# A fourth raw tile beside the gates, one-hot rows for four tokens at a time, and accumulating transfers for every second unit of the selection

## The chip, the cores and the metric

One core of one Trainium2 chip runs the whole program. The metric is the device time of one execution in microseconds, the median of the runs. The engines are named as in the profile: PE (TensorE, its matrix multiplications; PEld its weight loads), DVE (VectorE), ACT (ScalarE), POOL (GpSimd) and SP (SyncE, which issues most transfers). A transfer runs on the DMA engines; it is issued by a queue of SP or POOL.

## The reference

Two network blocks run over 256 tokens of width 1024 in fp32. The part that the change touches is the PEER layer, which occurs twice ("peer0", "peer1"):

```python
q = (xt @ w_q).reshape(T, 8, 2, 128)
s = jnp.einsum('thcd,hcnd->thcn', q, sub_keys)            # scores against 128 keys, two halves
s1, i1 = lax.top_k(s[:, :, 0], 16)
s2, i2 = lax.top_k(s[:, :, 1], 16)
cand_s = (s1[..., :, None] + s2[..., None, :]).reshape(T, 8, 256)
top_s, top_pos = lax.top_k(cand_s, 16)                    # 16 of 16384 experts per head and token
gates = jax.nn.softmax(top_s, axis=-1)
act = gelu(einsum('thkd,td->thk', u[expert_idx], xb))
out = einsum('thk,thkd->td', gates * act, v[expert_idx])
```

The other stages (an mLSTM mixer, latent attention, two feed-forward layers, a mixing layer of retention and neighbourhood attention) compute in fp32 as well.

## The kernel before

**Dense experts.** The kernel does not gather experts. For each of the 128 blocks of 128 experts it multiplies all 256 tokens with the block's u (`block(b)`, L499), applies gelu and stores the result in "big" (128 experts by 128 blocks by 256 tokens). A matrix of gates, zero where an expert is not chosen, is multiplied into "big", and the product with all of v (L556) is the output.

**Three passes.** Each fp32 product is made of three matmuls of fp32r parts: a number is split into a high part ("hi", a cast on ACT, L449) and the rest ("lo", a subtraction, L450). In a u-block, 16 matmuls read the high part of the weights and then 8 read the low part, so hi is needed about 1.9 us before lo.

**The stream of weights.** `Stream` carries all weights through the program in units of 128x1024 numbers (512 KB). `load` (L268) issues the transfer of a unit into a raw tile ("wraw", three of them) on SP's queue. `prep` makes hi and lo of it, two blocks ahead of use, in three pairs of tiles. The subtraction runs on DVE, or on POOL for units in `on_pool`. For a unit in `on_dma` there is no subtraction: `begin` (L300) lets ACT write the negated raw unit into one of two spare tiles (L306, tile "x1" or a name beginning with x), and POOL issues an accumulating transfer (L307) that adds the same unit from memory, in pieces: the copy is rounded to fp32r, so what is left in the tile is lo; the cast to hi follows in `prep` (L295). `fill` decides how far ahead that is begun, and `load_ahead` how far ahead is loaded:

```python
for i in range(self.done, self.done + (3 if self.done + 2 in self.borrow else 1)):
    if i in self.on_dma and i not in self.begun:
        self.begin(i)
...
while self.loaded < min(self.n, self.done + self.raw + (len(self.lent_raws) if self.loaded in self.borrow else 0)):
    self.load(self.loaded)
```

`lend` gives the stream more raw tiles for a range of units (`borrow`): in the selection, four pieces of "big" not yet written, for 44 units.

**One PEER layer.** First come 16 query units (`s_query`, `s_score`; in peer0 13 of them have their subtraction on POOL). Then 128 u-blocks run on PE, and beside them, on DVE, first the selection of the experts: `select` is a generator that yields the cost of each piece, and `spend(steps, 1.6)` lets each block take pieces up to that budget. When it is through, `Gates` starts in the same block (L943 to L949): `Gates.upto` calls `Gates.step` 67 times, spread evenly over the blocks that are left. A step joins the gates of four tokens to the finished blocks on DVE (L1688), makes one-hot rows in f16 on DVE (`make`, L1665 to L1668, four operations of 128x1024 for eight tokens, every second step, in one of two "hot" tiles), multiplies them on PE (`product`, L1678, eight matmuls for four tokens; two products after each other, every second step), and writes the gates of the blocks still to come on ACT (L1692). For the tokens whose gates are already in "big", gelu of a new block goes to a tile of its own, "gl" and a quarter of "x0" in turn (L1053), and DVE multiplies it in (`joins`, L1061); the other tokens go straight into "big" (L1056).

**Order.** DVE's instructions run in the order in which the code writes them. On PE, ACT, POOL and SP a planner with its own costs sets the order ahead of time, by due times and by what it thinks is ready; it is not the order of the code. `keep_in_program_order` ties an instruction behind the one before it in the code on the same engine.

Of the kernel before, what the change touches and what calls it, by code (L numbers as in the profile page):

```python
# [19 lines left out]
P = 128  # L20
# [18 lines left out]
FF_TAIL = 6  # L39
PACE = 4  # L40

SELECT, LENT = 44, 4

GATE_SCALE = 2.0 ** 15

# [183 lines left out]
class Stream:  # L229
# [38 lines left out]
    def load(self, i):  # L268
        n, w = (i - self.borrow.start) % (self.raw + len(self.lent_raws)) - self.raw, self.widths[i]
        t = self.lent_raws[n] if i in self.borrow and n >= 0 else self.tile(i, "raw", F32, self.raw)  # L270
        self.k.nc.sync.dma_start(out=t[:, :w], in_=self.src[i, :, :w])
        self.raws[i] = t

    def ring(self, i):
# [80 lines left out]
class Net:  # L355
# [292 lines left out]
    def mlstm(self, gain):  # L648
        nc, v, tc = self.nc, self.nc.vector, self.tc
        mm = nc.tensor.matmul  # L650
        with tc.tile_pool(name="ml", bufs=1) as pool, self.in_order():
# [196 lines left out]
                        (nc.gpsimd if ti else v).tensor_tensor(gog[:, ti], gog[:, ti], hng, op=ALU.mult)  # L848

            stages = [lambda h: None, s_decay, s_scores, s_turn, s_out, s_norm, s_keep]  # L850
            self.w.on_pool.update(range(self.w.i + 12, self.w.i + 40))
            for step, todo in enumerate(ML_BESIDE):
                todo = list(todo)
                if step == 2:
# [32 lines left out]
    def peer(self, layer, gain):  # L887
        nc, v, tc = self.nc, self.nc.vector, self.tc
        mm = nc.tensor.matmul
        with tc.tile_pool(name="pr", bufs=1) as pool:  # L890
# [20 lines left out]

            first = self.w.i + 16
            self.w.lend([self.room(big, n) for n in range(14, 14 + LENT)], range(first, first + SELECT))
            self.w.on_dma = set(range(self.w.i + 16 + 1, self.w.i + 16 + P - 8, 3))

            sc = self.scores_of(big)
            st = {}
# [22 lines left out]
            def block(b):  # L940
                ps = self.pp.tile([P, 512], F32, tag="acc", name=self.nm("ub"), bufs=4)
                self.cols_late(ps, self.xT, self.w.next())
                gates, start = now["gates"], now["start"]  # L943
                if start is not None:
                    gates.upto(b - 1, Gates.STEPS / (P - 2 - start))
                elif spend(steps, 1.6):
                    inner.close()
                    gates.pool = inner.enter_context(tc.tile_pool(name="gt", bufs=1))
                    now["start"] = b  # L949
                if b == P - 2:  # L950
                    gates.rest(b - 1)
                self.joins(late)
                if now["last"]:
                    self.activate(big, gates, late, *now["last"])
                now["last"] = b, ps
# [91 lines left out]
    def activate(self, big, gates, late, b, ps):  # L1047

        nc = self.nc
        t0 = gates.tokens if gates else 0  # L1050
        if t0:
            y = self.t(gates.pool, [P, S], "gl") if b % 2 else gates.room
            nc.scalar.activation(y[:, :t0], ps[:, :t0], AF.Gelu)  # L1053
            late.append((big[:, b, :t0], y[:, :t0]))
        if t0 < S:
            nc.scalar.activation(big[:, b, t0:], ps[:, t0:S], AF.Gelu)  # L1056
# [581 lines left out]
class Gates:  # L1638
# [1 line left out]

    TB = 8
    TJ = 4
    MADE = S // TB
    GROUPS = S // TJ
# [2 lines left out]
    def __init__(self, k, big, idx, g, iota):  # L1649
        self.k, self.big, self.idx, self.g = k, big, idx, g  # L1650
        x0 = k.t(k.gp, [P, 8, P, 2], "x0", F16)
        self.room = x0[:, 6:].rearrange("p a b c -> p (a b c)").bitcast(F32)
        self.iota, self.q = x0[:, self.TB // 2], x0[:, :self.TB // 2]
        k.nc.scalar.copy(self.iota, iota.unsqueeze(2).to_broadcast([P, P, 2]))
        self.pool = None
        self.tokens, self.n, self.owed = 0, 0, 0.0
        self.made, self.ps = {}, {}

    def make(self, m):
        k, tt, n = self.k, self.k.nc.vector.tensor_tensor, self.TB // 2  # L1660
        t = slice(m * self.TB, (m + 1) * self.TB)
        hot = k.t(self.pool, [P, 3, n, P, 2], "hot", F16, bufs=2)
        iota = self.iota.unsqueeze(1).to_broadcast([P, n, P, 2])
        on = lambda x: x[:, t].rearrange("p (a b) -> p a b", a=n).unsqueeze(2).to_broadcast([P, n, P, 2])
        tt(hot[:, 0], iota, on(self.idx[1]), op=ALU.is_equal)  # L1665
        tt(self.q, iota, on(self.idx[0]), op=ALU.is_equal)
        for p in range(2):
            tt(hot[:, 1 + p], self.q, on(self.g[:, p]), op=ALU.mult)  # L1668
        self.made[m] = hot
# [11 lines left out]
    def join(self, g, blocks, done):  # L1681
# [5 lines left out]
        if done and blocks:  # L1687
            nc.vector.scalar_tensor_tensor(dst, ps[:, :blocks], 1.0 / GATE_SCALE, dst, op0=ALU.mult, op1=ALU.mult)  # L1688
        if not done:
            assert self.k.w.done >= self.k.w.borrow.stop  # L1690
            if blocks < P:
                nc.scalar.mul(dst, ps[:, blocks:], 1.0 / GATE_SCALE)  # L1692
            self.tokens = (g + 1) * TJ
            self.ps.pop(g)

    def step(self, blocks):
        n = self.n
        self.n += 1
        join = 0 <= n - 3 < self.GROUPS
        if join:  # L1700
            self.join(n - 3, blocks, True)
        m, odd = divmod(n, self.TB // self.TJ)
        if m < self.MADE and not odd:
            self.make(m)
        if not odd:
            for g in (n - 2, n - 1):
                if 0 <= g < self.GROUPS:
                    self.product(g)
        if join:
            self.join(n - 3, blocks, False)  # L1710

# [11 lines left out]
def spend(steps, budget):  # L1723

    while budget > 0:
        c = next(steps, False)
        if c is False:
            return True
        if c is None:
            return False  # L1730
        budget -= c
    return False
# [59 lines left out]
```

## Time and profile before

| | |
|---|---|
| Median of 3 runs | 2618.07 us (2617.72 to 2621.56) |
| The profiled execution | 2626.37 us, span 2624.6 us |
| PE busy | 2551.2 us, 97% of the span |
| DVE busy | 1749.5 us, 67% |
| ACT busy | 1329.1 us, 51% |
| POOL busy | 259.6 us, 10% |

The profiled execution is 8.3 us longer than the median. Busy shares are an average over stages with different limits, so the stages are read one by one. For peer0 they are, in us from the start: the query stage 152.25 to 215.96; u-blocks 0 to 11, 215.96 to 251.21; blocks 12 to 35, 251.21 to 327.69; blocks 36 to 46, 327.69 to 359.97; blocks 47 to 127, in which gates are made, 359.97 to 633.15. In peer1 the query stage is 1133.12 to 1192.90 and blocks 47 to 127 are 1336.89 to 1611.59.

How to read the views: a timeline row is the start in us, the duration, engine, line and operation, out<-in with the shape, and how many consecutive ones the row joins; in brackets stands the idle time before it and what ended it. A row of the waits is the engine, tile and line that waited, for whom, the sum in us, how often, and the longest. A row of the groups has the count behind x, then busy time, mean ns of one, idle time before them and what ended it. A matmul's end is modelled, so that rows of PE overlap a little: starts are what to subtract. Some matmul records can be missing.

### The profile page before, as it was taken

The numbers are of one execution on the slowest core, as the hardware profiler recorded it, in microseconds if no ns is written. First come the engines' busy times: TensorE is split into PE (matmuls) and PEld (weight loads), VectorE is DVE, ScalarE is ACT, GpSimd is POOL, SyncE is SP. The second block draws the span as 40 slices with busy tenths as digits, with TensorE's granted clock in tenths as the row PEclk, the third lists the DMA queues.
The fourth block names the chain that finished last, engine by engine and source line by source line (L and its number), as shares of the span: only waits on it lengthen the run. The fifth ranks groups of instructions, "written<-read, shape, count | busy, mean of one in ns | idle before, by whom it ended". The sixth has DMA issues, their size and how long they took to land. (4 is left out here: it accounts for less than half of the span.)

```text
span 2624.6 us, 42853 instructions
## 1 busy us (share of the span) xinstructions
PE 2551.2 (97%) x16706; PEld 2303.7 (88%) x16706; DVE 1749.5 (67%) x3116; ACT 1329.1 (51%) x2109; POOL 259.6 (10%) x227
## 2 busy tenths in 40 slices
PE   8999999999999998999999999999999999999999
PEld 7789999999888887889999999888887998887898
DVE  6878966677555567679966677555566546666654
ACT  5445555555444445545555555444445444564543
POOL 0552000000000003010000000000011003001000
PEclk9999999999999999999999999999999999999999
DMA  7356777776555564367867776555565654554653
GB/s 246 109 194 194 217 194 209 209 203 223 201 192 193 193 207 159 118 204 206 224 186 201 206 211 224 194 193 193 193 201 192 223 162 169 180 178 153 208 194 105
DMA packets 139195, 502.42 MB, mean 191 GB/s; under 512 B 15832, under 2 KB 16088, under 8 KB 138992
## 3 DMA queue, kind: packets, MB, share of 16 engines
q1 hardware_dynamic: 122832, 443.93, 49.7%
q0 software_dynamic: 15440, 54.64, 11.1%
q8 instruction: 131, 2.15, 0.3%
q10 hardware_dynamic: 720, 1.11, 0.1%
q14 instruction: 72, 0.59, 0.1%
HBM read 494.38 MB, written 5.24 MB: 190 GB/s over the span
## 5 line engine op out<-in xcount | busy, mean ns | idle before, releaser
L450 DVE TENSOR_TENSOR wlo<-wraw,whi 128x1024 fp32r<-128x1024 f32 x446 | 547.1, 1228 | 499.2 <-ACT whi L449 498.2
L449 ACT CAST whi<-wraw 128x1024 fp32r<-128x1024 f32 x488 | 510.1, 1047 | 522.0 <-PE acc L556 319.9
L499 PE MATMUL ub<-xT,whi 128*128 128x256 f32 x4096 | 540.2, 285 | 4.6 <-ACT whi L449 4.4
L556 PE MATMUL acc<-whi,xT 128*128 128x512 f32 x1816 | 510.3, 394 | 12.3 <-ACT whi L449 7.3
L499 PEld LDWEIGHTS ub<-xT,whi 128*128 128x128 f32 x4096 | 507.9, 191 | 7.4 <-ACT whi L449 7.0
L556 PEld LDWEIGHTS acc<-whi,xT 128*128 128x128 f32 x1816 | 342.8, 190 | 85.9 <-ACT whi L449 7.3
L450 DVE TENSOR_TENSOR morelo<-wraw,morehi 128x1024 fp32r<-128x1024 f32 (+1 forms) x214 | 261.7, 1227 | 115.5 <-ACT morehi L449 115.1
L449 ACT CAST morehi<-wraw 128x1024 fp32r<-128x1024 f32 (+1 forms) x227 | 236.8, 1047 | 177.4 <-DMA wraw<-in_wst 71.6
L556 PE MATMUL acc<-wlo,xT 128*128 128x512 f32 x908 | 284.0, 393 | 0.2 <-DVE wlo L450 0.2
L556 PE MATMUL acc<-morehi,xT 128*128 128x512 f32 x808 | 234.2, 390 | 0.6 <-ACT morehi L449 0.6
L499 PE MATMUL ub<-xT,wlo 128*128 128x256 f32 x1408 | 200.2, 285 | 8.5 <-DVE wlo L450 8.0
L556 PEld LDWEIGHTS acc<-wlo,xT 128*128 128x128 f32 x908 | 172.5, 190 | 37.1 <-DVE wlo L450 0.9
L499 PEld LDWEIGHTS ub<-xT,wlo 128*128 128x128 f32 x1408 | 181.0, 191 | 13.3 <-DVE wlo L450 13.0
L556 PEld LDWEIGHTS acc<-morehi,xT 128*128 128x128 f32 x808 | 151.2, 188 | 32.3 <-ACT morehi L449 1.4
L450 POOL TENSOR_TENSOR wlo<-wraw,whi 128x1024 fp32r<-128x1024 f32 (+1 forms) x42 | 100.6, 2398 | 709.7 <-ACT whi L449 705.0
L455 PE MATMUL ps<-xT,whi 128*128 128x256 f32 (+1 forms) x552 | 160.9, 292 | 0.0
L456 PE MATMUL ps<-xT,whi 128*128 128x256 f32 (+1 forms) x552 | 159.2, 289 | 0.4 <-DVE xT L450 0.4
L457 PE MATMUL ps<-xT,wlo 128*128 128x256 f32 (+1 forms) x552 | 158.8, 288 | 0.0
L307 POOL DMA_DIRECT2D x<-in_wst x80 | 68.9, 862 | 759.2 <-ACT big L1056 228.7
L306 ACT ACTIVATE x<-wraw 128x1024 fp32r<-128x1024 f32 x64 | 67.8, 1060 | 138.7 <-DMA wraw<-in_wst 138.6
L556 PE MATMUL acc<-morelo,xT 128*128 128x512 f32 x404 | 128.4, 390 | 0.8 <-DVE morelo L450 0.8
L457 PE MATMUL ps<-xT,morelo 128*128 128x256 f32 x416 | 118.2, 284 | 2.3 <-POOL morelo L450 1.7
(498 smaller groups left out, 4213.6 us busy)
## 6 DMA issues: line engine op xcount, KB each, us to landing
wraw<-in_wst SPq DMA_DIRECT2D x768, 512.0 KB, 4.0
x<-in_wst POOLq DMA_DIRECT2D x80, 512.0 KB, 5.5
big<-in_wst SPq DMA_DIRECT2D x48, 512.0 KB, 5.3
wraw<-in_wst SPq DMA_DIRECT2D x10, 384.0 KB, 3.3
sp<-x SPq DMA_DIRECT2D x4, 512.0 KB, 3.0
big<-in_keys POOLq DMA_DIRECT2D x8, 256.0 KB, 7.5
sp<-big SPq DMA_DIRECT2D x4, 512.0 KB, 7.7
x<-sp POOLq DMA_DIRECT2D x4, 512.0 KB, 4.8
```

The costliest lines, as they stand in the source:

```text
L306: k.nc.scalar.mul(lo[:, :w], self.raws[i][:, :w], -1.0)
L307: k.nc.gpsimd.dma_start(out=lo[:, :w], in_=self.src[i, :, :w], accum_op=ALU.add)
L449: self.nc.scalar.copy(hi, src)
L450: (self.nc.gpsimd if pool else self.nc.vector).tensor_tensor(lo, src, hi.bitcast(F32), op=ALU.subtract)
L455: mm(ps, a[0], b[0], start=start, stop=False)
L456: mm(ps, a[0], b[1], start=False, stop=False)
L457: mm(ps, a[1], b[0], start=False, stop=stop)
L499: mm(ps[:, :S], w[of][:, k], xT[part][:, k], start=n == 0, stop=n == len(steps) - 1)
L556: mm(acc[ti][h], a, w[b][:, h * 512:(h + 1) * 512], start=first, stop=last)
```

## The change

In the selection, every second unit instead of every third gets its lo by an accumulating transfer (20 units of the first 40, then 27, so 47 instead of 40 per layer); the four lent tiles serve 40 units instead of 44, and a block takes pieces of the selection up to a budget of 1.75. In the gates' stretch a new tile "wraw" is lent as a fourth raw tile, for all units up to the end of u; since `fill` looks at `borrow`, accumulations may there be begun up to three units ahead. One-hot rows are made for four tokens in each step (four operations of 128x512, in one of three tiles), and one product follows each step. "gl" is replaced by a second quarter of "x0", which smaller one-hot rows leave free; the tile sizes add up to the same. All transfers of `load` are tied to program order on SP. In the query stage of peer0 the subtractions that POOL did move to DVE: the range for POOL ends with the mLSTM's own units.

```diff
-SELECT, LENT = 44, 4
+SELECT, LENT = 40, 4
...
-        self.k.nc.sync.dma_start(out=t[:, :w], in_=self.src[i, :, :w])
+        self.k.tc.keep_in_program_order(self.k.nc.sync.dma_start(out=t[:, :w], in_=self.src[i, :, :w]))
...
-            self.w.on_pool.update(range(self.w.i + 12, self.w.i + 40))
+            self.w.on_pool.update(range(self.w.i + 12, self.until))
...
-            self.w.on_dma = set(range(self.w.i + 16 + 1, self.w.i + 16 + P - 8, 3))
+            self.w.on_dma = set(range(first + 1, first + SELECT, 2)) | set(range(first + SELECT + 1, first + P - 8, 3))
...
-                elif spend(steps, 1.6):
+                elif spend(steps, 1.75):
                     inner.close()
                     gates.pool = inner.enter_context(tc.tile_pool(name="gt", bufs=1))
                     now["start"] = b
+                    gates.lent = first + SELECT
+                    raw = self.t(gates.pool, [P, UNIT], "wraw")
+                    self.w.lend([raw], range(max(self.w.loaded, first + SELECT), first + P))
...
-            y = self.t(gates.pool, [P, S], "gl") if b % 2 else gates.room
+            y = gates.rooms[b % 2] if b < P - 1 else self.t(gates.pool, [P, UNIT], "wraw")
...
-    TB = 8
+    TB = 4
...
-        self.room = x0[:, 6:].rearrange("p a b c -> p (a b c)").bitcast(F32)
+        self.rooms = [x0[:, n:n + 2].rearrange("p a b c -> p (a b c)").bitcast(F32) for n in (4, 6)]
...
-        hot = k.t(self.pool, [P, 3, n, P, 2], "hot", F16, bufs=2)
+        hot = k.t(self.pool, [P, 3, n, P, 2], "hot", F16, bufs=3)
...
-            assert self.k.w.done >= self.k.w.borrow.stop
+            assert self.k.w.done >= self.lent
...
-        m, odd = divmod(n, self.TB // self.TJ)
-        if m < self.MADE and not odd:
-            self.make(m)
-        if not odd:
-            for g in (n - 2, n - 1):
-                if 0 <= g < self.GROUPS:
-                    self.product(g)
+        if n < self.MADE:
+            self.make(n)
+        if 0 <= n - 2 < self.GROUPS:
+            self.product(n - 2)
```

## Rows read from the trace of the kernel before

**Rows 1.** By stretch: us, busy PE, PEld, DVE, ACT, POOL; PEclk, DMA share, GB/s.
```profile
152.25:215.96 63.71, 59.23 (x475) 58.71 (x474) 44.53 (x126) 31.64 (x69) 36.22 (x20) 0.95 0.65 201
251.21:327.69 76.48, 72.18 (x579) 69.76 (x578) 73.49 (x245) 43.20 (x60) 7.69 (x9) 1.00 0.78 218
359.97:633.15 273.18, 267.98 (x2458) 264.06 (x2456) 190.75 (x326) 150.34 (x331) 20.69 (x24) 1.00 0.72 203
1133.12:1192.90 59.78, 58.10 (x474) 57.58 (x474) 44.66 (x139) 31.52 (x69) 4.97 (x7) 0.97 0.68 213
1336.89:1611.59 274.70, 267.97 (x2458) 264.05 (x2456) 190.80 (x326) 151.15 (x331) 20.62 (x24) 1.00 0.71 203
```

**Rows 2.** PE in time order: blocks 19 and 20; blocks 77 to 79.
```profile
274.15 2.08 PE L499 MATMUL ub<-xT,whi 128*128 128x256 f32 x16
277.03 2.08 PE L499 MATMUL ub<-xT,whi 128*128 128x256 f32 x16
...
461.52 2.08 PE L499 MATMUL ub<-xT,whi 128*128 128x256 f32 x16
...
465.31 2.16 PE L499 MATMUL ub<-xT,whi 128*128 128x256 f32 x16
...
468.26 2.08 PE L499 MATMUL ub<-xT,whi 128*128 128x256 f32 x16
```

**Rows 3.** PE's waits: blocks 47 to 127 of peer0; then its query stage.
```profile
PE ps L1678 <- DVE hot L1668: 3.8, 9, 0.6
PE ub L499 <- ACT whi L449: 1.2, 2, 0.8
...
PE ps L456 <- DVE klo L450: 2.0, 1, 2.0
```

**Rows 4.** ACT in time order, one round of three units in the gates' stretch.
```profile
441.62 1.06 ACT L306 ACTIVATE x<-wraw 128x1024 fp32r<-128x1024 f32 x1 [1.97 <-DMA wraw<-in_wst]
...
442.89 1.05 ACT L449 CAST whi<-wraw 128x1024 fp32r<-128x1024 f32 x1
...
445.85 1.04 ACT L295 CAST whi<-wraw 128x1024 fp32r<-128x1024 f32 x1
...
451.93 1.06 ACT L306 ACTIVATE x<-wraw 128x1024 fp32r<-128x1024 f32 x1 [1.96 <-DMA wraw<-in_wst]
```

**Rows 5.** DVE's groups by form, blocks 47 to 127 of peer0.
```profile
L450 DVE TENSOR_TENSOR wlo<-wraw,whi 128x1024 fp32r<-128x1024 f32 x58 | 71.0, 1224 | 81.7 <-ACT whi L449 81.5
L1668 DVE TENSOR_TENSOR hot<-x,gT 128x1024 f16<-128x1024 f16 x62 | 40.1, 689 | 1.1
```

**Rows 6.** DVE in time order, a small operation of the gates' stretch.
```profile
387.37 0.17 DVE L1061 TENSOR_TENSOR big<-gl,big 128x16 f32<-128x16 f32 x1
```

**Rows 7.** POOL and DVE in time order, query stage of peer0; then DVE, peer1.
```profile
160.55 2.34 POOL L450 TENSOR_TENSOR wlo<-wraw,whi 128x1024 fp32r<-128x1024 f32 x1 [5.01 <-ACT whi L449]
...
161.10 2.33 DVE L450 TENSOR_TENSOR klo<-big,khi 128x128 fp32r<-128x128 f32 x3
...
1140.81 0.69 DVE L450 TENSOR_TENSOR klo<-big,khi 128x128 fp32r<-128x128 f32 x3
```

**Rows 8.** Transfers, 216 to 330 us: packets, MB, engines' share; issues, median us to landing.
```profile
q1 hardware_dynamic: 5130, 18.68, 46.0%
q0 software_dynamic: 1592, 5.80, 30.4%
...
x<-in_wst POOLq DMA_DIRECT2D x12, 512.0 KB, 6.7
```

**Rows 9.** ACT in time order, four units at the start of the selection.
```profile
222.68 1.06 ACT L306 ACTIVATE x<-wraw 128x1024 fp32r<-128x1024 f32 x1
...
224.59 1.05 ACT L449 CAST whi<-big 128x1024 fp32r<-128x1024 f32 x1 [0.58 <-ACT big L1056]
...
227.43 1.05 ACT L449 CAST whi<-big 128x1024 fp32r<-128x1024 f32 x1 [1.51 <-PE ub L499]
...
230.36 1.05 ACT L295 CAST whi<-wraw 128x1024 fp32r<-128x1024 f32 x1 [1.59 <-PE ub L499]
```

## The prediction

> **What bounds the kernel now.** Read the busy times by stretch first [rows 1]: TensorE is busy for 72.18 of 76.48, for 267.98 of 273.18 us, and so on, so the span is TensorE's own work and the few places where it waits. The change leaves that work alone but for the order of some matmuls; what it can move is the waits. The second row is 24 of the 128 query-key blocks (12 to 35) while experts are selected: 76.48 us, VectorE busy 73.49, so VectorE is the limit there. The third is blocks 47 to 127 of peer0, in which the gates are made: 273.18 us with VectorE busy for 190.75 and the DMA engines for 0.72, so nobody is full, and yet TensorE waits. The first and fourth rows are the query stages of the two peers, which do the same work in 63.71 and 59.78 us.
>
> How large is the loss in the gates' stretch? One block of 24 matmuls lasts 2.88 us unhindered (blocks at 274.15 and 277.03) [rows 2]. Block 77 starts at 461.52, is followed by 16 one-hot products, and block 78 starts at 465.31, 3.79 later; block 79 starts at 468.26, 2.95 later. So a group of 16 products costs 0.91 + 0.07 = 0.98 us. 81 blocks and 32 groups need 81 x 2.88 + 32 x 0.98 = 264.6 us; the stretch took 273.18 and, in peer1, 274.70 [rows 1]. The loss is 8.6 and 10.1 us, 18.7 in all. The list of waits names, in peer0, the products' operand "hot" from VectorE (3.8 us, 9 times) and the ScalarE cast (1.2 us) [rows 3]; the rest is waits too short for that list.
>
> Both come from one loop. Follow ScalarE in time order [rows 4]: it idles 1.97 us for a raw tile, copies it at 441.62 (L306, the negated copy that an accumulating transfer will complete), and only then casts the unit that TensorE wants next, at 442.89. The cast of the copied unit itself ends at 446.89 (445.85 + 1.04); that frees its tile, the next load into it is issued and lands, and the next copy starts on its landing at 451.93, 5.04 after the tile came free. Every third unit is copied, and three tiles turn in the same beat, so it is always this one tile: 451.93 - 441.62 = 10.31 us for three blocks, where TensorE needs 264.6/81 x 3 = 9.80. VectorE's subtraction, and the one-hot rows queued behind it in VectorE's fixed order, inherit the delay; this is why "hot" is named.
>
> **The change, part by part.**
> *Fourth raw tile.* With four tiles the copied unit i no longer follows itself: its tile is freed by unit i-4, an uncopied one, when VectorE has subtracted (1.22 us [rows 5] after the cast). If the copy keeps its place, one cast ahead, the loop is: cast 1.05, subtract 1.22, load 5.04, copy 1.06, 0.2 to the next cast (442.68 to 442.89): 8.57 us per three blocks, under 9.80. The stall goes; what is late next is TensorE itself. Small collisions stay: I keep 2.5 us per peer, between 0 and all of it. Gain 18.7 - 5.0 = 13.7. If the cover is thinner than that, the two uneven things left are the product groups and the moment at which a load lands.
>
> *Four tokens at a time.* 64 visits of 8 products instead of 32 of 16. The trace holds only groups of 16; a group costs 0.98, of which 0.07 is the slower block behind it. If all 0.98 is proportional to the matmuls the split is free; if the 0.07 is paid per visit, it is 32 x 0.07 = 2.2 us per peer. I take 2.1 per peer, 4.2 in all; ends 0 and 4.5. On the other side it spreads the products: three blocks now hold one or two groups of 16, later two or three of 8, which makes the loop's need steadier; counted at nothing. For VectorE, the four operations of 128x1024 take 0.69 each now [rows 5]; halves are not in the trace. Bounds: half of that and all of it. An operation with next to no elements takes 0.17 [rows 6], so half the size is about 0.17 + (0.69 - 0.17)/2 = 0.43: 64 x 4 x 0.43 = 110 us against 31 x 4 x 0.69 = 85, so 25 us more in a stretch where VectorE has 273 - 191 = 82 free. Hidden, unless a half stays at 0.65 or more. The Trainium skill speaks against this part: "VectorE: DVE Perf Modes", section "The TRN2 errata", says that each VectorE operation on SBUF pays a fixed extra term, measured there as about 150 cycles, so that many small operations pay it many times; 128 more operations would by that page be an estimated 20 us per peer. The trace agrees in kind (0.17 us for 16 elements), and by the page the sum would be the same, since it lies in free time.
>
> *No lo on GpSimd in peer0's query stage, and loads in a fixed order.* GpSimd does 13 of these subtractions now and is busy 36.22 us in peer0's query stage against 4.97 in peer1's [rows 1]. While one of them runs (160.55, 2.34 us), VectorE needs 2.33 us for three key subtractions that take 0.69 in peer1 [rows 7]; TensorE waits 2.0 us for such a subtraction [rows 3]. The 13 go to VectorE; that it has room is seen in peer1, where VectorE does all of them and is busy 44.66 of 59.78, as long as now in peer0 [rows 1]. The Trainium skill, "SBUF — State Buffer", section "Who interferes with whom", states the cause as a rule: a VectorE operation with two inputs in SBUF and a GpSimd operation lock one shared port pair against each other; the rows agree (0.69 becomes 2.33). At best peer0 becomes peer1: 63.71 - 59.78 = 3.9 us; at worst nothing. I take 3.3: the wait of 2.0 and two thirds of the other 1.9. The fixed order of loads also holds back lent loads that float ahead now; every load then waits for the one before it on SP's queue. I count it in the 3.3, ends 0.
>
> *Selection: every second unit by accumulation, four blocks less of lent tiles, a larger budget.* VectorE spends 73.49/24 = 3.06 us per block now [rows 1]: two of three units cost it 1.22, so 0.82, and 2.25 is selection. The budget 1.75 for 1.6 makes that 2.25 x 1.094 = 2.46, the halved subtraction 0.61, together 3.07. VectorE's pace stays; selection ends at block 43 x 1.6/1.75 = 39 to 40. The transfers pay: in the first blocks of selection 12 accumulations took 30.4% of 114 us, 2.9 us each, and 36 loads 46.0%, 1.46 each [rows 8]. A block then asks for 1.46 + 1.45 = 2.91 us of all 16 DMA engines, above TensorE's 2.88. Blocks 12 to 35 run at 3.19 (76.48/24), so transfers fit there; in the some 18 others of the stretch they may not. Ends: 2 us gained per peer (fewer slow blocks) and 18 x (2.91/0.9 - 2.88) = 6 lost. I take 1 lost per peer, 2 in all, nearest to VectorE's unchanged row. The "gl" tile's place is taken by halves of x0 that nothing else uses: no new wait.
>
> **Sum**: -13.7 + 4.2 - 3.3 + 2 = -10.8. The profiled execution has 2626.37 us round a span of 2624.6, so it becomes 2615.6; the median of the runs, 2618.07, lies 8.3 below it and becomes 2607.
>
> **The rivals.**
> *B, the copy moves too far ahead.* The new lending range also switches the look-ahead of the accumulations from one unit to three. Where it is three now, in the selection, the order is visible [rows 9]: copy from "wraw" at 222.68, casts at 224.59 and 227.43, and then, at 230.36, the cast of that copied tile. The copy stands two casts ahead. There seven tiles hold units long landed; with four, ScalarE would stand before the copy until the load has come, with two casts behind it, and TensorE, VectorE's subtraction and the one-hot rows behind those. The loop becomes 8.57 + a second cast of 1.05 + what stands between two casts, from 0.2 to the 1.9 between 443.94 and 445.85, where ScalarE's part of the gates waits for VectorE [rows 4]: 9.8 to 11.5 us against 9.80. Where the loop is 10.6 it is 0.8 x 29 rounds = 23 us of stall per peer instead of 9.3: 28 more for two, with 4.2 and 2 on top and 3.3 off, 31 slower; where it is 10.2, 0.4 x 29 = 12 per peer, 8 slower. It decides from about 10.1, a gap of 0.5; middle of the two, 19 slower, 2637. For it: the order in rows 9. Against: with one unit of look-ahead the copy was put where the tile lands, not where the code first asks, so a late tile may push it back behind a cast.
> *C, nothing to measure.* The products' wait is VectorE's own: subtract, join and four one-hot operations stand in one order. Then only the cast's share goes, 1.2 of 5.0 listed us [rows 3], so 0.24 x 18.7 = 4.5: -4.5 + 4.2 - 3.3 + 2 = -1.6, 2616.5. For it: 3.8 of the 5.0 are "hot". Against: VectorE idles 81.5 us for the cast in that stretch [rows 5].
> *D, the accumulations limit the selection.* Two spare tiles serve every second unit: copy 1.06, 0.9 of GpSimd issue, transfer, cast and TensorE's use come round in four blocks, 11.5 us. At the 6.7 us measured now [rows 8] there is about 1.5 left, so it decides from a landing of 8.2 us. If it grows to 9.5 the round is 12.8, 0.33 more a block, 40 x 0.33 = 13 per peer less what the slow blocks hide (24 x 0.31 = 7.4): +11 for both, 2618.
>
> **How the numbers follow.** Forecast 0.50, B 0.32, C 0.13, D 0.05. The measurement can tell about 0.2%, 5 us. Faster by more: the forecast, 0.50; within: C and D, 0.18; slower: B, 0.32. The forecast's own range is 2596 (stalls all gone, the split free, 2 gained in the selection) to 2616. For 8 in 10 the range must take in C, D and the half of B up to its middle and a little over: 2596 to 2640.
>
> **What would show it.** Right: in the gates' stretch ScalarE's idle time before L306 shrinks from some 2 us a copy to little, loss per peer under 4 us, "hot" waits nearly gone, VectorE's one-hot operations near 0.43 us, peer0's query stage near 60 us without GpSimd. Wrong, by B: the copy stands before two casts and idles for its load, blocks come later than 10 us for three. Wrong, by D: accumulations landing over 8 us in the selection and blocks 0 to 11 above 2.88 us.

## The result: slower by 1.5%

The changed kernel takes 2657.27 us (median of 4 runs, 2653.64 to 2658.19) against 2617.89 for the kernel before (2614.26 to 2621.56). The ratio is 1.0148, with a 95% interval of 1.013 to 1.0165: 39 us slower, where 2607 was forecast and the range ended at 2640.

The profile after, busy time by stretch, with the columns of [rows 1]. The rows are, for peer0, the query stage, blocks 0 to 46 and blocks 47 to 127, and then the same for peer1:

```profile
148.94:208.77 59.83, 57.30 (x475) 56.44 (x475) 45.07 (x140) 31.58 (x69) 4.67 (x7) 1.00 0.55 188
208.77:356.48 147.71, 141.10 (x1158) 138.24 (x1158) 128.23 (x408) 90.99 (x129) 18.76 (x22) 1.00 0.89 243
356.48:644.15 287.67, 271.23 (x2444) 264.10 (x2441) 195.56 (x443) 153.19 (x331) 20.72 (x24) 1.00 0.69 193
1143.77:1201.79 58.02, 56.98 (x475) 56.37 (x475) 44.79 (x139) 31.58 (x69) 4.55 (x7) 1.00 0.53 184
1201.79:1348.71 146.92, 140.69 (x1159) 138.16 (x1158) 128.18 (x408) 91.00 (x129) 18.65 (x22) 1.00 0.88 244
1348.71:1639.79 291.08, 272.82 (x2444) 265.59 (x2441) 196.11 (x443) 153.78 (x332) 20.63 (x24) 0.99 0.69 192
```

Set the third and the last row beside [rows 1]: the gates' stretch, which the change was expected to shorten, went from 273.18 to 287.67 and from 274.70 to 291.08 us, 30.9 us more. Blocks 0 to 46 of peer0 took 144.01 us before:

```profile
215.96:359.97 144.01, 139.71 (x1142) 137.29 (x1142) 131.83 (x403) 83.78 (x122) 12.05 (x14) 1.00 0.76 212
```

They take 147.71 now, of which 1.0 is products that begin earlier. The query stages are shorter. The two profiled executions differ by less than the medians (27.3 us of span): the one of before was 8.3 us above its median, and part of the shorter query stage of peer0 is its clock, 0.95 before and 1.00 after.

Where PE waited in the gates' stretches, peer0 and then peer1, shows what changed its name:

```profile
PE ub L499 <- ACT whi L449: 16.2, 17, 2.7
...
PE ub L499 <- ACT whi L449: 17.1, 19, 1.9
```

The "hot" waits of [rows 3] are gone from the list; what PE waits for now is the cast, and for up to 2.7 us at a time. ACT in time order says why, over one round of three units:

```profile
462.00 1.04 ACT L295 CAST whi<-wraw 128x1024 fp32r<-128x1024 f32 x1
...
466.17 1.06 ACT L306 ACTIVATE x<-wraw 128x1024 fp32r<-128x1024 f32 x1 [2.03 <-DMA wraw<-in_wst]
467.13 1.03 ACT L449 CAST whi<-wraw 128x1024 fp32r<-128x1024 f32 x1
...
469.83 0.35 ACT L1695 ACTIVATE big<-ps 128x212 f32<-128x212 f32 x1 [1.32 <-DVE big L1691]
470.07 1.04 ACT L449 CAST whi<-wraw 128x1024 fp32r<-128x1024 f32 x1
...
473.39 1.04 ACT L295 CAST whi<-wraw 128x1024 fp32r<-128x1024 f32 x1
...
477.05 1.06 ACT L306 ACTIVATE x<-wraw 128x1024 fp32r<-128x1024 f32 x1 [2.27 <-DMA wraw<-in_wst]
```

Compare [rows 4]: there one cast stood between the copy (L306) and the cast of the copied unit (L295), here two stand there. ACT idles 2.03 us for the load, copies, and only then makes the cast at 467.13 that PE is waiting for. PE's row, and then DVE with the rest of the round:

```profile
468.21 2.17 PE L499 MATMUL ub<-xT,whi 128*128 128x256 f32 x16 [1.22 <-ACT whi L449]
...
468.19 1.23 DVE L450 TENSOR_TENSOR wlo<-wraw,whi 128x1024 fp32r<-128x1024 f32 x1 [2.85 <-ACT whi L449]
469.33 0.46 DVE L1691 SCALAR_TENSOR_TENSOR big<-ps,big 128x300 f32<-128x300 f32 x1
...
471.34 1.22 DVE L450 TENSOR_TENSOR wlo<-wraw,whi 128x1024 fp32r<-128x1024 f32 x1
```

Walk round it: the copy at 466.17, a cast at 467.13, then 1.9 us before the next cast, 1.32 of them idle, because ACT's write of the gates waits for the join on DVE (469.33), which itself stands behind the subtraction at 468.19; a second cast at 470.07; its subtraction ends at 472.56 and frees the tile; the load into it takes until the next copy at 477.05, 4.49 us. The round is 10.88 us for three blocks, and that is the usual one: over the 24 copies of each peer's stretch the median from copy to copy is 10.88 and 10.87. What PE needs is 2.88 a block, and 3.40 for one with a visit of eight products, as two starts in time order show that nothing disturbs:

```profile
356.48 2.16 PE L499 MATMUL ub<-xT,whi 128*128 128x256 f32 x16
...
359.88 2.15 PE L499 MATMUL ub<-xT,whi 128*128 128x256 f32 x16
```

So a visit costs 0.52, and blocks 47 to 127 with 62 visits need 81 x 2.88 + 62 x 0.52 = 265.5 us. The loss is 22.2 and 25.6 us per peer, where it was 8.6 and 10.1. That is the place and the loop of the prediction's rival B, and the whole is a good deal dearer than B's middle; whether the cause that B names, the look-ahead, is behind it is tested below.

### The profile page after: what moved, and what is told of

Read it like the earlier page. It is cut to its first block, busy times and chain, and to the rows that moved or that the text cites. A ratio compares the mean times of both kernels' runs of the same rounds, so it can differ in the third digit from the quotient of the medians.

```text
span 2651.9 us, 43144 instructions
## 1 busy us (share of the span) xinstructions
PE 2555.7 (96%) x16706; PEld 2299.6 (87%) x16706; DVE 1757.1 (66%) x3376; ACT 1351.0 (51%) x2127; POOL 238.9 (9%) x227
## 5 line engine op out<-in xcount | busy, mean ns | idle before, releaser
L450 DVE TENSOR_TENSOR wlo<-wraw,whi 128x1024 fp32r<-128x1024 f32 x456 | 559.1, 1227 | 518.5 <-ACT whi L449 517.6
L449 ACT CAST whi<-wraw 128x1024 fp32r<-128x1024 f32 (+1 forms) x484 | 504.7, 1044 | 502.1 <-PE acc L556 318.4
L499 PE MATMUL ub<-xT,whi 128*128 128x256 f32 x4096 | 547.6, 287 | 33.5 <-ACT whi L449 33.2
L499 PE MATMUL ub<-xT,wlo 128*128 128x256 f32 x1296 | 183.7, 284 | 11.4 <-DVE wlo L450 11.3
L499 PEld LDWEIGHTS ub<-xT,wlo 128*128 128x128 f32 x1296 | 166.8, 191 | 15.8 <-DVE wlo L450 15.6
L307 POOL DMA_DIRECT2D x<-in_wst x94 | 81.0, 862 | 831.9 <-ACT x L306 298.0
L306 ACT ACTIVATE x<-wraw 128x1024 fp32r<-128x1024 f32 x72 | 76.2, 1058 | 119.3 <-DMA wraw<-in_wst 117.5
L450 POOL TENSOR_TENSOR wlo<-wraw,whi 128x1024 fp32r<-128x1024 f32 (+1 forms) x28 | 67.1, 2401 | 683.0 <-ACT whi L449 682.0
```

The lines of the kernel that those rows point to most:

```text
L306: k.nc.scalar.mul(lo[:, :w], self.raws[i][:, :w], -1.0)
L307: k.nc.gpsimd.dma_start(out=lo[:, :w], in_=self.src[i, :, :w], accum_op=ALU.add)
L449: self.nc.scalar.copy(hi, src)
L450: (self.nc.gpsimd if pool else self.nc.vector).tensor_tensor(lo, src, hi.bitcast(F32), op=ALU.subtract)
L499: mm(ps[:, :S], w[of][:, k], xT[part][:, k], start=n == 0, stop=n == len(steps) - 1)
```

## The experiments

Kernels whose name begins with a_ start from the changed kernel, those with b_ from the kernel before, and the two "best" from before as well. Ratios are to the kernel before, measured on the same chip; the last two columns are the length of blocks 47 to 127 in the profile.

| run | us | ratio (95%) | peer0 | peer1 |
|---|---|---|---|---|
| before | 2617.89 | 1 | 273.18 | 274.70 |
| changed kernel | 2657.27 | 1.0148 (1.013 to 1.0165) | 287.67 | 291.08 |
| a_copy_pin2 | 2608.14 | 0.9945 (0.9925 to 0.9965) | 265.58 | 266.05 |
| a_copy_pin1 | 2613.27 | 0.9939 (0.9916 to 0.9963) | 267.07 | 269.39 |
| a_three_tiles | 2631.05 | 1.0040 (1.0021 to 1.0059) | 273.05 | 275.22 |
| b_tb4_4th_ahead1 | 2650.73 | 1.0101 (1.0078 to 1.0124) | 286.46 | 286.61 |
| b_tb4 | 2626.33 | 1.0006 (0.9989 to 1.0022) | 276.88 | 270.83 |
| b_nodma_gates | 2603.27 | 0.9932 (0.9915 to 0.9950) | 264.59 | 264.59 |
| b_sel | 2620.53 | 1.0002 (0.9990 to 1.0015) | 268.28 | 269.20 |
| b_query | 2623.41 | 0.9994 (0.9981 to 1.0006) | 275.94 | 277.52 |
| b_pin | 2625.94 | 0.9998 (0.9982 to 1.0013) | 275.35 | 277.63 |
| best2 | 2606.08 | 0.9916 (0.9887 to 0.9946) | 264.59 | 264.59 |
| best1 | 2593.58 | 0.9864 (0.9842 to 0.9886) | 264.89 | 264.90 |

The kernel before had medians of 2620.8, 2624.5 and 2629.1 us in the three series of runs, so kernels of different series are compared by ratio. b_query and b_pin leave the code of the gates' stretch as it was, and it took 275.4 to 277.6 us there: differences of 2 to 3 us in the last two columns are not to be read.

### The copy one place later

a_copy_pin2 ties the copy beside the gates to the order of the code, begun two units ahead:

```diff
-        k.nc.scalar.mul(lo[:, :w], self.raws[i][:, :w], -1.0)
+        copy = k.nc.scalar.mul(lo[:, :w], self.raws[i][:, :w], -1.0)
+        if len(self.lent_raws) == 1:
+            k.tc.keep_in_program_order(copy)
...
-        for i in range(self.done, self.done + (3 if self.done + 2 in self.borrow else 1)):
+        for i in range(self.done, self.done + (2 if len(self.lent_raws) == 1 else 3 if self.done + 2 in self.borrow else 1)):
```

> The changed kernel with one thing altered: in the gates' stretch the negated copy is tied to the order of the code, so that it stands one cast ahead of its own unit's cast and not two. Tiles, transfers, one-hot rows and selection stay. Theory 1 (the copy that waits for its load holds back two casts; round of 10.9 us for three blocks): the round falls to what TensorE needs, about 10.1 with the products, the loss beside the gates from some 24 and 27 us per peer to under 8, the time to 2612 to 2630 us. Theory 2 (64 visits and twice as many one-hot operations are the loss): no change from the changed kernel's 2657, at least 2648.

It came out at 0.9945, 2608 us, below the range that was expected. The order of instructions on SP, POOL, DVE and PE is that of the changed kernel, instruction for instruction; only ACT's differs, by these copies, each of which stands behind one more cast (and by five small writes of the gates per peer, which stand ahead of a cast where they stood behind it). ACT in time order:

```profile
464.05 1.05 ACT L451 CAST whi<-wraw 128x1024 fp32r<-128x1024 f32 x1 [1.41 <-PE ub L501]
466.35 1.06 ACT L306 ACTIVATE x<-wraw 128x1024 fp32r<-128x1024 f32 x1 [1.25 <-DMA wraw<-in_wst]
...
467.85 1.06 ACT L451 CAST whi<-wraw 128x1024 fp32r<-128x1024 f32 x1
...
470.85 1.05 ACT L295 CAST whi<-wraw 128x1024 fp32r<-128x1024 f32 x1
...
474.25 1.05 ACT L451 CAST whi<-wraw 128x1024 fp32r<-128x1024 f32 x1 [1.48 <-PE ub L501]
475.50 1.06 ACT L306 ACTIVATE x<-wraw 128x1024 fp32r<-128x1024 f32 x1 [0.21 <-DMA wraw<-in_wst]
```

The copy still waits 1.25 us for its load, but what stands behind it is one cast only, and the casts before it wait for PE ("PE ub"), not PE for them. By stretch, with the columns of [rows 1]:

```profile
360.17:625.75 265.58, 265.58 (x2444) 262.69 (x2441) 199.50 (x446) 156.47 (x332) 20.76 (x24) 1.00 0.75 211
1331.30:1597.35 266.05, 265.85 (x2444) 262.75 (x2441) 198.95 (x444) 155.39 (x332) 20.65 (x24) 1.00 0.74 211
```

PE is busy for all of 265.58 us: the loss beside the gates is gone. One place in ACT's order is worth 22.1 + 25.0 = 47.1 us beside the gates, and 1.0148 against 0.9945 in the whole.

a_copy_pin1 goes on one place further, so that the copy stands directly before its own cast:

```diff
-        for i in range(self.done, self.done + (3 if self.done + 2 in self.borrow else 1)):
+        for i in range(self.done, self.done + (1 if len(self.lent_raws) == 1 else 3 if self.done + 2 in self.borrow else 1)):
```

> The changed kernel with the negated copy beside the gates held back further: after the cast of the unit before, so directly ahead of its own unit's cast. Theory 1 (what matters is how many casts stand behind a copy that waits for its load): the copy now holds back only its own cast, no stall from that, but its accumulation starts 2 to 3 us later and lands some 6 us after the copy, about when TensorE wants the low part: between 2600 and 2625. Rival (the copy has to be early, two casts ahead was right and the load is just late): above 2640.

0.9939, not to be told from a_copy_pin2. Each copy now finds its load landed: ACT's idle time before it is 0.0 us at all 46 of them in blocks 47 to 127, where it was about 2 us in the changed kernel. So the copy need not be early, and it does harm where it stands ahead of other casts before its load has landed.

### Who moved the copy

a_three_tiles leaves the fourth tile out of the changed kernel:

```diff
-                    raw = self.t(gates.pool, [P, UNIT], "wraw")
-                    self.w.lend([raw], range(max(self.w.loaded, first + SELECT), first + P))
```

> The changed kernel without the fourth raw tile: the lending line is gone, three tiles turn as before, all else stays as changed. Theory 1 (the fourth tile moved the copy, nothing else did): the copy is one cast ahead again, the loss beside the gates falls from some 24 and 27 us per peer to about the 8.6 and 10.1 of the kernel before, and with the selection's 5 us and the visits' 4 us the time is 2618 to 2632. Theory 2 (the loss is in the four-token one-hot rows, and the tile helps): above 2657.

1.0040, 2631, within the range of theory 1; blocks 47 to 127 take what they took before. The order on SP, POOL, DVE and PE is again that of the changed kernel, and on ACT the copies stand one cast ahead. So more than two thirds of the loss hangs on the tile. The kernel is still slower than the kernel before by some 10 us, though no other part alone costs anything that can be measured (below). Two pieces are seen in its profile. Blocks 0 to 46 lose 6.7 us in the two peers (2.0 of them products that begin earlier), as with the selection's part alone, but the gates' stretch does not win that back as it does there. The other is in the list of PE's waits over the whole program, the first matmuls of v, both peers together, before

```profile
PE acc L556 <- ACT x L449: 2.3, 2, 1.1
```

and in a_three_tiles:

```profile
PE acc L556 <- ACT x L449: 4.7, 2, 2.4
```

In the changed kernel that wait is 5.3 us, in a_copy_pin2 2.3 again. It comes with the four-token rows: b_tb4, which has these alone, has 4.8, and b_sel 2.4.

b_tb4_4th_ahead1 adds to the kernel before only the four-token rows and the fourth tile, and keeps the look-ahead at one unit:

```diff
-        for i in range(self.done, self.done + (3 if self.done + 2 in self.borrow else 1)):
+        for i in range(self.done, self.done + (3 if self.done + 2 in self.borrow and len(self.lent_raws) > 1 else 1)):
```

> The kernel before with four-token one-hot rows and the fourth raw tile, and with a look-ahead of one unit beside the gates as before; selection, query stage and the order of loads stay. Theory 1 (the fourth tile alone makes the planner put the copy two casts ahead, whatever the look-ahead): rounds near 10.9 us, loss beside the gates over 20 us per peer, 2640 to 2662. Rival (it was the look-ahead of three, as the prediction's rival B has it): the copy one cast ahead, loss under 6 us per peer, 2604 to 2618.

1.0101, 2651: theory 1. ACT in time order:

```profile
474.79 1.06 ACT L306 ACTIVATE x<-wraw 128x1024 fp32r<-128x1024 f32 x1 [3.20 <-DMA wraw<-in_wst]
475.76 1.03 ACT L449 CAST whi<-wraw 128x1024 fp32r<-128x1024 f32 x1
...
478.70 1.04 ACT L449 CAST whi<-wraw 128x1024 fp32r<-128x1024 f32 x1
...
481.86 1.04 ACT L295 CAST whi<-wraw 128x1024 fp32r<-128x1024 f32 x1
...
485.83 1.06 ACT L306 ACTIVATE x<-wraw 128x1024 fp32r<-128x1024 f32 x1 [2.04 <-DMA wraw<-in_wst]
```

Two casts between copy and own cast, a round of 11.04 us, with a look-ahead of one. So the look-ahead of three, which the prediction named as the cause in its rival B, is not needed for it. Compared with b_tb4 (1.0006), which lacks only the tile, the order on SP, POOL, DVE and PE is the same, and on ACT only the copies beside the gates have moved. The programs say the same before they run: the changed kernel built with a look-ahead of one has the same order on every engine as with three, and so has the kernel before, whose copies stay one cast ahead with either. It is the tile that the planner answers to. That it believes the load has landed by then is the natural reading; its own times are not in any profile, so this is not shown.

### What the loss before hung on

b_nodma_gates leaves the accumulations beside the gates out, so that DVE makes all low parts there:

```diff
-            self.w.on_dma = set(range(self.w.i + 16 + 1, self.w.i + 16 + P - 8, 3))
+            self.w.on_dma = set(range(first + 1, first + SELECT, 3))
```

> The kernel before with accumulating transfers in the first 44 units only; beside the gates all low parts are made by VectorE, some 25 more per peer, 31 us more on 191 of 273. No copy, no wait for one. Theory (the whole loss beside the gates, 8.6 and 10.1 us, hangs on the copy that stands before a cast): PE's waits there vanish, 2597 to 2606. Rival (the loss hangs on VectorE's order: subtraction, join, one-hot rows): more work there makes it worse, 2622 to 2650.

0.9932, 2603, as the theory had it:

```profile
357.14:621.73 264.59, 264.59 (x2458) 263.01 (x2456) 217.36 (x349) 129.60 (x305) 0.00 (x0) 1.00 0.47 163
1324.62:1589.21 264.59, 264.58 (x2458) 263.00 (x2456) 217.33 (x349) 129.53 (x305) 0.00 (x0) 1.00 0.47 162
```

With three tiles and with 26.6 us more of work on DVE (190.75 in [rows 1], 217.36 here), PE waits for nothing: 264.59 us, which is the 264.6 that the prediction had worked out as its need. So the waits for "hot" in [rows 3] were not for want of time on DVE; they were inherited from the copy.

### The other parts, one at a time

Four-token rows with three tiles (b_tb4; `TB = 4`, three "hot" tiles, one product a step, y in two quarters of x0):

> The kernel before with four-token one-hot rows alone, three raw tiles and a second quarter of x0 for gelu; the fourth tile's place stays empty. Theory (64 visits cost 0.07 us each more, VectorE's extra 25 us are hidden): 2 us per peer more in products, 2618 to 2626. Rival (the copy's loop meets a steadier need, so stalls shrink): 2608 to 2616. Second rival (twice as many one-hot operations delay the subtraction): above 2630.

1.0006: nothing to be measured. The blocks 47 to 127 of peer0, to be read beside the third of [rows 1]:

```profile
363.97:640.85 276.88, 269.79 (x2458) 264.44 (x2456) 201.59 (x452) 150.80 (x331) 20.75 (x24) 1.00 0.71 200
```

DVE is busy for 10.8 us more, not for 25. The selection's part (b_sel):

```diff
-SELECT, LENT = 44, 4
+SELECT, LENT = 40, 4
...
-            self.w.on_dma = set(range(self.w.i + 16 + 1, self.w.i + 16 + P - 8, 3))
+            self.w.on_dma = set(range(first + 1, first + SELECT, 2)) | set(range(first + SELECT + 1, first + P - 8, 3))
...
-                elif spend(steps, 1.6):
+                elif spend(steps, 1.75):
```

> The kernel before with the selection's part alone: accumulations for every second of the first 40 units, four lent tiles for 40 units, a budget of 1.75. Theory (DMA engines are full in the selection, the block loses what the shorter selection wins): 4 to 6 us slower in all, 2621 to 2627. Rival (transfers fit, the selection ends earlier): 2612 to 2618. Rival D (two spare tiles limit the round): above 2630.

1.0002: between the theory and its rival. The blocks up to 46 lose 3.7 us in peer0, as in the changed kernel, and the gates' stretch, which has three blocks more for the same steps, wins some 5 back.

The query stage without GpSimd (b_query):

```diff
-            self.w.on_pool.update(range(self.w.i + 12, self.w.i + 40))
+            self.w.on_pool.update(range(self.w.i + 12, self.until))
```

> The kernel before with one edit: GpSimd makes no low part in peer0's query stage, VectorE makes the 13. Theory (GpSimd's subtraction and VectorE's hold each other up): the wait of 2.0 us for the key subtraction goes, three such subtractions take 0.7 us and not 2.3, the query stage of peer0 comes to about 61 us, the time 2 to 4 us less. Rival (the stage waits for transfers): the stage stays at 63 to 64, no change in the time.

DVE in time order, the query stage of peer0 by stretch,

```profile
157.30 0.69 DVE L450 TENSOR_TENSOR klo<-big,khi 128x128 fp32r<-128x128 f32 x3
...
149.91:211.41 61.50, 58.77 (x476) 57.91 (x475) 44.97 (x140) 31.84 (x69) 5.32 (x7) 0.97 0.69 217
```

and PE's waits in it:

```profile
PE ps L455 <- ACT q L449: 1.5, 1, 1.5
...
PE ps L456 <- DVE klo L450: 0.3, 1, 0.3
```

The wait goes as expected: three key subtractions take 0.69 us and not 2.33 [rows 7], and PE waits 0.3 us for one where it waited 2.0. But it now waits 1.5 us for the query's own high part, and the stage wins little. It took 61.5 us where it had taken 63.7, but at a granted clock of 0.97 instead of 0.95. b_nodma_gates has this stage unchanged, GpSimd's subtractions and the wait of 2.0 us included, and in its profile the clock was 0.97 as well:

```profile
151.25:213.14 61.89, 58.32 (x475) 57.80 (x475) 44.79 (x126) 31.86 (x69) 36.47 (x20) 0.97 0.65 209
```

At the same clock, then, the edit is worth some 0.4 us. Whether the clock is a gain of the edit too is not shown: it was 0.95 in four of the five profiles in which this stage is unchanged, and 0.97 or more in all seven with the edit. The time, 0.9994 with an interval of 0.9981 to 1.0006, can't tell either from nothing. The Trainium skill, "SBUF — State Buffer", section "Who interferes with whom", has a VectorE operation with two inputs in SBUF and a GpSimd operation lock one shared port pair against each other; with GpSimd out of the stage the lengthening is gone, which agrees.

Loads in program order (b_pin; the one line of `load`):

> The kernel before with one edit: the loads of weights are tied to the code's order on SP's queue. Theory (lent loads that float ahead cost little): within 2 us of before either way. Rival (they crowd out the keys and early units of the query stage): the first wait of 2.3 us in peer0's query stage shrinks, 2 to 4 us less.

0.9998, as the theory had it, but for another reason: peer0's query stage came to 59.9 us, and blocks 0 to 11 took 38.3 and 41.2 us in the two peers instead of 35.25. By stretch, the query stage and blocks 0 to 11 of peer0, then blocks 0 to 11 of peer1:

```profile
151.21:211.11 59.90, 58.09 (x476) 57.73 (x475) 45.46 (x126) 30.17 (x66) 35.65 (x19) 0.97 0.55 185
211.11:249.43 38.32, 36.53 (x297) 35.58 (x297) 32.91 (x122) 23.52 (x34) 3.57 (x5) 1.00 0.83 237
1190.44:1231.67 41.23, 37.38 (x296) 36.93 (x296) 32.89 (x122) 23.85 (x33) 4.27 (x5) 0.96 0.82 230
```

DVE and PE keep the order of before; what moved are the loads on SP, of which the lent ones had floated ahead, and one early copy per peer with its accumulation. What one stage wins the next one pays.

### A version that beats both

best2 is b_nodma_gates with the two edits of b_query and b_pin. best1 also spreads the selection over more blocks:

```diff
-SELECT, LENT = 44, 4
+SELECT, LENT = 50, 4
...
-                elif spend(steps, 1.6):
+                elif spend(steps, 1.4):
```

> The kernel before without accumulations beside the gates (2603 by the run of that alone), and with the changed kernel's two edits to the query stage and to the order of loads. Theory: the parts add, the query stage gives 1 to 4 us: 2599 to 2604 where before is 2618 to 2621. Rival (the query stage gives nothing by itself, as its own run had it): 2602 to 2606.

> As best2, and the selection is spread over more blocks: a budget of 1.4 for 1.6 and lent tiles for 50 units. VectorE then has 2.25 x 1.4/1.6 + 0.82 = 2.79 us of work per block, less than TensorE's 2.88, so the 7.3 us lost per peer in blocks 12 to 35 should go, while the gates' 79 blocks still have VectorE room. Theory: 8 to 14 us faster than best2, 2586 to 2595. Rival (pieces of the selection are uneven, the stalls stay or the gates' shorter stretch gives them back): 2598 to 2606.

best2 has 0.9916, no better than b_nodma_gates alone within their intervals, so the query edits stay unproven. best1 has 0.9864, 1.4% faster than the kernel before: in its rows

```profile
212.67:352.63 139.96, 138.62 (x1140) 136.89 (x1140) 127.05 (x394) 86.64 (x123) 13.79 (x16) 1.00 0.85 241
352.63:617.52 264.89, 264.89 (x2461) 263.31 (x2459) 221.60 (x352) 128.78 (x301) 0.00 (x0) 1.00 0.49 160
```

blocks 0 to 46 take 139.96 us where they took 144.01, and blocks 47 to 127 have no loss although the gates are made in fewer blocks: DVE had the room there all along. Against best2, of the same series, it is 12.5 us faster, within the 8 to 14 of its theory. The budget went the opposite way to the change's 1.75.

## Why the prediction was wrong

**The step that failed** is the condition in the fourth tile's part: "If the copy keeps its place, one cast ahead". It didn't: it went two casts ahead, and the round that was worked out as 8.57 us took 10.88. Under that condition the sum came out: a_copy_pin2, which is the changed kernel with the copy in that place, has 0.9945 (0.9925 to 0.9965), and the prediction's 2607 is 0.9958 of the median before. The round is then PE's own, 265.58/81 x 3 = 9.84 us (two copies above stand 9.15 apart); of the 5.0 us kept as a remainder, 0.6 were needed (265.58 and 266.05 against 265.5). The terms were less right than their sum, and that much is luck: the tile gave 18.1 us where 13.7 was taken, and blocks 0 to 46 cost some 5 where 2 was.

**The weighing that led there.** The trace of before had the evidence: [rows 9] show the copy two casts ahead where more than three tiles turn. It was put down to the look-ahead of three units, and held against it that "with one unit of look-ahead the copy was put where the tile lands". There, both the tiles and the look-ahead differ from the gates' stretch, so the trace alone could not tell them apart; the runs did, with one unit of look-ahead and with three. So B deserved more than 0.32, and the forecast less than 0.50.

**B's price.** Its bounds, 9.8 to 11.5 us a round, hold the 10.88 and 11.04 that were seen; for its two cases 10.2 and 10.6 were taken. The mis-sized term is "what stands between two casts", 0.2 to 1.9. It is 1.9 in both rounds shown, and with reason: once the round is late, ACT's step of the gates waits for DVE's join, which waits for the subtraction, which waits for the first of the two casts, so the gap is part of the round. The number of rounds was wrong the other way: 29 were counted, but [rows 1] have 24 accumulations in the stretch (POOL x24). In the case of 10.6 the two errors cancel, and its 23 us of stall per peer lie by the 22.2 and 25.6 measured. The time lies 17 us beyond the range because the range took in B only to a little over its middle, 2637, half way between the cases of 10.2 and 10.6; the case of 10.6 alone comes to 2649.

**Point by point.**
- What bounds the kernel: right. PE's need was computed as 264.6 us and is 264.59 when nothing disturbs it. Rival C fell with the same run.
- Four tokens at a time: 62 visits of eight cost 0.52 each (3.40 - 2.88), so 64 cost 33.3 against 31.4 for 32 of sixteen, 1.9 us per peer where 2.1 was taken. VectorE's halves were put at 0.43 us, and 25 us more of work; groups by form show

```profile
L1671 DVE TENSOR_TENSOR hot<-x,gT 128x512 f16<-128x512 f16 x126 | 47.9, 421 | 2.1
```

  0.42. Two sizes give the fixed part of an operation's length: 2 x 0.42 - 0.69 = 0.15 us. The Trainium skill, "VectorE: DVE Perf Modes", section "The TRN2 errata", has a fixed term of about 150 cycles, by an estimate from its clock 0.156 us; the lengths agree. What 128 more operations cost does not follow from it: b_tb4's DVE is busy for 201.59 us instead of 190.75 [rows 1], 10.8 more, where the prediction had 25 and its estimate by the page 20. An operation begins before the one ahead of it has ended: from start to start two of 128x512 stand 0.34 us apart and two of 128x1024 0.61, so that 2 x 0.34 - 0.61 = 0.07 us is paid for each. All of it is hidden.
- Query stage: 3.3 us taken; 2.2 seen in the stage's length (63.7 to 61.5), of which some 0.4 at the same clock. The difference of 3.9 us between the two peers, from which the 3.3 was taken, held a difference of clock, 0.95 against 0.97 [rows 1], and of PE's other waits. That the fixed order of loads costs nothing was right in sum and wrong in detail: it wins in the query stage and loses in the blocks behind.
- Selection: 2 us taken, 0 measured by itself. The transfers are fuller, as the prediction feared. The view of transfers from 209 to 323 us of the changed kernel, to be read beside [rows 8], and then its accumulations from 208.77 to 245.18, blocks 0 to 11:

```profile
q0 software_dynamic: 2685, 9.82, 47.5%
...
x<-in_wst POOLq DMA_DIRECT2D x18, 512.0 KB, 8.0
...
x<-in_wst POOLq DMA_DIRECT2D x6, 512.0 KB, 8.6
```

  The 8.0 us is a mixture: 8.6 in blocks 0 to 11, and 5.1 to 5.4 for most of those issued from 265 us on. In blocks 0 to 11 the DMA engines' share is 1.00:

```profile
208.77:245.18 36.41, 36.02 (x296) 35.41 (x296) 33.72 (x135) 23.54 (x33) 4.94 (x6) 1.00 1.00 276
```

  That is 3.03 us a block where 2.91/0.9 = 3.23 was the worst end (no row stands behind the 0.9), and 36.41 us for twelve blocks that took 35.25. With the selection's part alone (b_sel) the share there is 0.84, with the fixed order of loads alone (b_pin) 0.83; it takes both to fill the engines. Rival D's 8.2 was passed in these blocks, and yet PE waited only 0.3 us for an accumulated tile there: D did not set the pace.
- The whole: in the two profiles, 22.2 + 25.6 - 8.6 - 10.1 = 29.1 for the stall, 3.8 for the visits and 6.6 - 2.0 = 4.6 in blocks 0 to 46 make 37.5, and everything else went the other way (the query stages 5.6 us shorter, in part by their clock), so that the spans differ by 27.3. The medians differ by 39.4. The two profiled executions lie some 8 above and 4 below their medians, so what lies outside the u-blocks, the 3.0 where u ends (5.3 - 2.3) among it, can't be weighed to a few us.

**What stays open.** Why the planner moves the copy when a tile is added was read from orders, not from its times. Why PE waits 2 to 3 us longer for the first matmuls of v with four-token rows (b_tb4, a_three_tiles, the changed kernel), and not in a_copy_pin2, was not tried by itself. Why the selection's part costs nothing alone and some 7 us together with the four-token rows (a_three_tiles) is open too.

## What to carry to other kernels

An instruction that waits for a transfer holds up everything behind it on its engine, here by about 2 us at each copy: when a buffer is added, look at where an automatic order puts the instruction that consumes the transfer, and tie it down if work with a nearer due time stands behind it. One place in one engine's order was worth 2% here, more than all the sizes in the change together. And before making a transfer earlier, ask whether the engine that it relieves is short at all: beside the gates VectorE had 82 us to spare, and without the transfers that spared it 27 the whole loss was gone.

## What the runs showed of the hardware

In blocks 0 to 11 of the two peers the share of the 16 DMA engines went from 0.72 and 0.74 before to 1.00 and 1.02 in the changed kernel, in this mix of loads and accumulations. They then moved 276 and 281 GB/s, where it was 206 and 209, and the landing of an accumulation lengthened at the median from 6.5 and 6.7 us to 8.6 and 8.1.

On VectorE two one-hot operations of 128x512 last 0.42 us each and start 0.34 us apart, so that the length of an operation overstates what one more costs.

After PE's wait of 2.9 us for the first operand of v in peer0, the granted clock of the changed kernel was 0.55 and 0.60 in the next two stretches of 2 us, so mostly at the lower of its two levels (1.2 GHz), and the first ten matmuls of v took 4.0 us where they took 2.4 before; after the wait of 2.4 us in peer1 it stayed at 1.00.
